# One order of all engines for a whole encoder block, in place of a framework's order and a local planner

## The chip, the cores and the metric

The kernel runs on one NeuronCore of a Trainium2 chip. Five engines work side by side, each through its own queue of instructions, in order: TensorE (PE: matmuls and transposes), VectorE (DVE), ScalarE (ACT), GpSimd (POOL) and SyncE (SP), which only issues transfers. Sixteen DMA engines move data between memory and the core. Engines wait for one another through semaphores. The metric is the device time of one execution in microseconds (us), as the median of several runs.

## The reference, cut to what matters

One block of an encoder, for 256 tokens of 2048 channels in float32, and 256 memory tokens:

```python
h = rms_norm(x, g_mix); proj = h @ w_in                      # latents (512 + 256 + 64) and dq, dk, dv (1024 each)
q = rms_norm(c_q, g_q_lat) @ w_uq; kv = rms_norm(c_kv, g_kv_lat) @ w_ukv
out_mla = mla_attention(...)                                 # 8 heads, rope on 64 channels
o_diff = diff_attention(...)                                 # 4 heads, p1 - lam * p2, then rms_norm
x = x + concat(out_mla, out_diff) @ w_out
xq = rms_norm(x, g_xattn) @ w_xq                             # cross attention, 4 heads
hm = rms_norm(mem, g_mem); xk, xv = hm @ w_xk, hm @ w_xv
x = x + softmax(xq xk^T) xv @ w_xo
hf = rms_norm(x, g_ffn)
x = x + (silu(hf @ w_gate) * (hf @ w_up)) @ w_down           # hidden width 5632
return rms_norm(x, g_final)
```

## The kernel before, in words

**Arithmetic.** Every float32 operand is split in two reduced-precision parts, high and low (`split_into`, L214): ScalarE casts the high part, VectorE subtracts it from the source to get the low part. One product is three matmuls: high by high, high by low, low by high (`mm`, L198; `mm_late`, L204, puts the products that need the low part of the weights last). A matmul has 128 by 128 weights in the array and 512 moving columns at most. Each piece of weights is loaded as float32 by SP into one of three buffers (`wraw`, 1 MB each) and split into one of four pairs of buffers (`wh`, `wl`).

**Tiling.** The 256 tokens are two row tiles (`tt`), an output column block is 512 wide (`oc`). The wide products take weights in pairs of 256 input rows by 1024 output columns. Some pairs are taken plainly ("P": 24 matmuls), some in a form with sums of blocks and seven products in place of eight ("W": 21 matmuls, more additions on VectorE). `GU_KINDS` and `DN_KINDS` say which. The sums of the weights are in `tsum`, those of the activations in `forms`; four banks q1, q5, q7, q6 gather the products, and VectorE joins them.

**Stages.** Latent projections (L546 on), attention, `w_out`, cross attention, then the FFN: a narrow chunk of 512 hidden columns (`narrow_chunk`, L1000: `ga` is the gate projection, `ua` the up projection, `sg` its SiLU, `h` the product of both, and between `ga` and `ua` `normalized_pairs` (L972) scales the transposed activations `x2T_f` by the row `rrow`, for which two transposes `rps` are made, and splits them into `x2n` and `forms`), then five wide chunks of 1024, with three down projections for them, and the final norm.

**Buffers.** Most activations live in one pool, `act`, with 24 slots of 4 KB per partition; accumulators in two pools of four banks each (`pacc`, `pps`), which change roles after each wide product (`banks.reverse()`).

**What sets the order before.** Three ways, one after the other.
- Up to and with the narrow chunk, the framework's scheduler orders the instructions from the order of the source, its own model of times, and what each reads and writes. Transfers on SP are kept in the order of the source (`tc.keep_in_program_order`).
- The wide chunks are not called directly. `flow_project`, `flow_add`, `flow_chunk` (L1083 to L1342) make a list of operations by hand (`Flow.op`, L103), each with its engine, a duration from a table (`V_COLS`, `S_COLS`, L43), what it needs, and rings of buffers that it takes and gives (`Ring`, `Hold`). `Flow.emit` (L112) keeps TensorE's matmuls in the order of the source, works back from it by when each operation is wanted, and then runs a list schedule: at each step, of the operations of an engine that could start within 0.3 us of its earliest one, the one wanted first. TensorE is taken to begin 10 us after the others. The result is issued in a block in which the framework keeps the order given.
- The rest (last part of the down projection, final norm, output) is again the framework's.

POOL makes constants at the start, the rope angles, some powers (`rstd_of`, L304) and two kinds of transfers: the memory tokens (`mn`, L921, four loads of 512 KB, for the sums of squares of `mem`, which are needed to scale `xk` and `xv`), and the final gain (`gfb`, L1385).

Of the kernel before, what the change touches and what calls it, by code (L numbers as in the profile page):

```python
# [11 lines left out]
F32 = mybir.dt.float32  # L12
# [30 lines left out]
V_COLS, S_COLS = {1024: (1.136, 1.218), 512: (0.602, 0.684), 256: (0.336, 0.416), 128: (0.202, 0.282)}, \  # L43
    {1024: (0.954, 1.053), 512: (0.523, 0.621), 256: (0.265, 0.368)}
PASS, PASS_LAG, TURN, LOADED = 0.2267, 0.2, 0.108, (4.8, 2.75)

# [22 lines left out]
class Ring:  # L69


    def __init__(self, n):
        self.n, self.holds = n, []


class Hold:


    def __init__(self, ring):
        self.gives = []  # L80
        before = ring.holds[-ring.n] if len(ring.holds) >= ring.n else None
        self.after = before.gives if before else []
        ring.holds.append(self)


class Op:


    def __init__(self, engine, busy, lag, fn, need, take, transfer):
        self.engine, self.busy, self.lag, self.fn, self.transfer = engine, busy, lag, fn, transfer  # L90
        self.need, self.take = [n for n in need if n is not None], take
        self.before, self.then, self.wanted, self.ready, self.left = [], [], 1e9, 0.0, 0


class Flow:
# [4 lines left out]
    def __init__(self):  # L100
        self.ops, self.chains = [], {}

    def op(self, engine, busy, lag, fn, need=(), take=(), give=(), chain=None, transfer=0.0):  # L103
        o = Op(engine, busy, lag, fn, need, take, transfer)
        for h in give:
            h.gives.append(o)
        if chain is not None:
            self.chains.setdefault(chain, []).append(o)
        self.ops.append(o)
        return o  # L110

    def emit(self, started):  # L112
        for o in self.ops:
            o.before = [(n, True) for n in o.need] + [(g, True) for h in o.take for g in h.after]
        for chain in self.chains.values():
            for x, y in zip(chain, chain[1:]):
                y.before.append((x, False))
        for o in self.ops:
            o.left = len(o.before)
            for b, data in o.before:  # L120
                b.then.append((o, data))
        t = 0.0
        for o in self.chains["PE"]:
            o.wanted, t = t, t + o.busy
        sorted_ops, left = [o for o in self.ops if not o.left], {o: o.left for o in self.ops}
        for o in sorted_ops:
            for n, _ in o.then:
                left[n] -= 1
                if not left[n]:
                    sorted_ops.append(n)  # L130
        assert len(sorted_ops) == len(self.ops)
        for o in reversed(sorted_ops):
            for n, data in o.then:
                o.wanted = min(o.wanted, n.wanted - (o.lag + self.HANDOVER if data else 0.0))
        place = {o: i for i, o in enumerate(self.ops)}
        open_ops, free, queue = {}, dict(started), 0.0
        for o in self.ops:
            if not o.left:
                open_ops.setdefault(o.engine, []).append(o)
        for _ in self.ops:  # L140
            picked = None
            for engine, ops in open_ops.items():
                if not ops:
                    continue
                f = free.get(engine, 0.0)
                soon = min(max(f, o.ready) for o in ops) + self.CHOICE
                o = min((o for o in ops if max(f, o.ready) <= soon), key=lambda o: (o.wanted, place[o]))
                start = max(f, o.ready)
                if picked is None or start < picked[0]:
                    picked = start, o  # L150
            start, o = picked
            open_ops[o.engine].remove(o)
            free[o.engine] = start + o.busy
# [4 lines left out]
            o.fn()  # L158
            for n, data in o.then:
                n.ready = max(n.ready, end + self.HANDOVER if data else start + o.busy)  # L160
                n.left -= 1
                if not n.left:
                    open_ops.setdefault(n.engine, []).append(n)
# [17 lines left out]
@with_exitstack  # L181
def encoder_block(ctx: ExitStack, tc: tile.TileContext, a, out):
    nc = tc.nc
    PS = bass.MemoryType.PSUM
    const = ctx.enter_context(tc.tile_pool(name="const", bufs=1))
    wp = ctx.enter_context(tc.tile_pool(name="wp", bufs=3))
    act = ctx.enter_context(tc.tile_pool(name="act", bufs=24))
    sb = ctx.enter_context(tc.tile_pool(name="sb", bufs=2))
    small = ctx.enter_context(tc.tile_pool(name="small", bufs=4))
    pacc = ctx.enter_context(tc.tile_pool(name="pacc", bufs=4, space=PS))  # L190
# [177 lines left out]
    def wide_project(pairs, src, order, kinds, leave, join, closed=(0, 1), before=None, seed=None, carried=()):  # L368
# [3 lines left out]
        if seed is not None:  # L372
            for tt in range(NT):
                for oc in range(2):
                    nc.scalar.copy(out=accs[tt][oc], in_=seed(tt, oc))
# [1141 lines left out]
```

## Time and profile before

| | |
|---|---|
| median of 3 runs | 1145.73 us (1145.5 to 1145.84) |
| the profiled execution | 1144.28 us |
| its span, first to last instruction | 1142.5 us |
| TensorE busy | 1127.7 us, 99% of the span, 5360 matmuls and transposes |
| VectorE busy | 1014.8 us, 89% |
| ScalarE busy | 694.6 us, 61% |
| moved by DMA | 222.16 MB, mean 194 GB/s |
| mean granted TensorE clock | 0.996 |

Busy time is the time in which an engine has at least one instruction in work. Matmuls follow one another before the one ahead has ended, so a busy TensorE isn't always one at its full rate. Rows of the order of time show: start, length in us, engine, line, operation, output <- inputs, shape, count, and in brackets the idle time of the engine before it and what ended that. A "PEld" is a load of weights into the array. Rows of groups show: line, engine, operation, tiles, shape, count, then busy us and mean ns of one, then the idle time before them. Rows of queues show packets, MB and the share of the time of all 16 DMA engines.

### The profile page before, as it was taken

The page shows a single profiled execution, that of the slowest core. Times are in us where ns is not written, and L with a number is a line of the kernel's source. Part 1 is how long each engine was busy: PE and PEld are TensorE (multiplying, and loading weights), DVE is VectorE, ACT ScalarE, POOL GpSimd, SP SyncE. Part 2 cuts the span into 40 slices and gives each one's busy share as a digit, 9 for nine tenths or more (in the row PEclk, how much of TensorE's full clock was granted, in tenths as well). Part 3 has the DMA queues.
Part 4 walks back from the last instruction along what each step waited for, and adds up shares of the span by engine and source line. Part 5 has one row for each costly group of instructions (what it writes and reads, how often), then busy time and mean ns, then how long its engine had stood idle before and what let it go on. Part 6 is the DMA issues. An engine that isn't in the chain of part 4 may idle for free.

```text
span 1142.5 us, 14716 instructions
## 1 busy us (share of the span) xinstructions
PE 1127.7 (99%) x5360; PEld 941.6 (82%) x5360; DVE 1014.8 (89%) x1378; ACT 694.6 (61%) x999; POOL 56.4 (5%) x75
## 2 busy tenths in 40 slices
PE   9999999999999999899999999999999999999997
PEld 7888888888888888688888888888888888888876
DVE  7788766878896776999999999999999999999995
ACT  7755455567566555656675566666665665756752
POOL 4910000000001000000000000000000000000000
PEclk9999999999999999999999999999999999999999
DMA  9655333446557445455556465456455554656453
GB/s 357 245 193 187 123 127 139 178 143 232 211 225 258 148 147 184 148 184 211 197 183 223 182 221 221 158 210 221 171 204 215 190 217 183 216 219 229 166 184 129
DMA packets 35497, 222.16 MB, mean 194 GB/s; under 512 B 4320, under 2 KB 5600, under 8 KB 11104
## 3 DMA queue, kind: packets, MB, share of 16 engines
q1 hardware_dynamic: 33696, 216.60, 52.2%
q0 software_dynamic: 864, 3.15, 0.8%
q10 hardware_dynamic: 864, 1.47, 0.4%
q8 instruction: 42, 0.69, 0.2%
q14 instruction: 31, 0.25, 0.1%
HBM read 219.11 MB, written 2.10 MB: 194 GB/s over the span
## 4 chain that ended last, share of the span: by engine, by line
PE 84%; DVE 11%; issue 3%; ACT 1%; DMA 1%; POOLq 0%; POOL 0%; SPq 0%; DVEq 0%; ACTq 0%
PE acc L1042 11%; PE acc L1041 11%; PE acc L1039 11%; PE acc L200 8%; PE acc L201 8%; PE acc L202 8%; DVE wl L1053 4%; PE q L1039 3%; PE q L1042 3%; PE q L1041 3%; PE acc L207 2%; PE acc L208 2%; PE acc L210 2%; PE pt L616 1%; DVE tsum L1136 1%
## 5 line engine op out<-in xcount | busy, mean ns | idle before, releaser
L1050 ACT CAST wh<-wraw 128x1024 fp32r<-128x1024 f32 x242 | 228.2, 957 | 95.4 <-PE acc L1042 64.5
L1053 DVE TENSOR_TENSOR wl<-wraw,wh 128x1024 fp32r<-128x1024 f32 x242 | 261.1, 1100 | 5.6 <-ACT wh L1050 3.5
L217 DVE TENSOR_TENSOR wl<-wraw,wh 128x1024 fp32r<-128x1024 f32 (+3 forms) x159 | 187.0, 1187 | 57.4 <-ACT wh L216 54.7
L216 ACT CAST wh<-wraw 128x1024 fp32r<-128x1024 f32 (+3 forms) x159 | 158.9, 1012 | 118.3 <-PE acc L202 76.0
L1050 ACT CAST wh<-tsum 128x1024 fp32r<-128x1024 f32 x108 | 113.7, 1054 | 114.1 <-DVE tsum L1131 51.4
L1053 DVE TENSOR_TENSOR wl<-tsum,wh 128x1024 fp32r<-128x1024 f32 x108 | 131.7, 1220 | 6.0 <-ACT wh L1050 5.4
L1041 PE MATMUL acc<-wh,x2n_h 128*128 128x512 f32 x320 | 125.6, 392 | 3.5 <-ACT sg L1009 2.8
L1042 PE MATMUL acc<-wh,x2n_l 128*128 128x512 f32 x320 | 124.9, 390 | 0.0
L201 PE MATMUL acc<-wl,x0T_h 128*128 128x512 f32 x224 | 88.7, 396 | 0.0
L202 PE MATMUL acc<-wh,x0T_l 128*128 128x512 f32 x224 | 88.3, 394 | 0.0
L200 PE MATMUL acc<-wh,x0T_h 128*128 128x512 f32 x224 | 86.8, 396 | 0.3 <-DVE x0T_h L220 0.3
L1039 PE MATMUL acc<-wl,x2n_h 128*128 128x512 f32 x320 | 85.8, 390 | 0.0
L1041 PE MATMUL q<-wh,forms_h 128*128 128x512 f32 x216 | 84.5, 391 | 0.3 <-ACT wh L1050 0.3
L1042 PE MATMUL q<-wh,forms_l 128*128 128x512 f32 x216 | 84.2, 390 | 0.0
L1039 PE MATMUL q<-wl,forms_h 128*128 128x512 f32 x216 | 75.9, 392 | 1.1 <-DVE wl L1053 0.9
L1136 DVE TENSOR_TENSOR tsum<-tsum,wraw 128x512 f32<-128x512 f32 x108 | 74.0, 686 | 0.5
L1041 PEld LDWEIGHTS acc<-wh,x2n_h 128*128 128x128 f32 x320 | 60.4, 189 | 16.7 <-ACT sg L1009 3.2
L1042 PE MATMUL acc<-wh,hT_l 128*128 128x512 f32 x184 | 71.7, 390 | 0.0
L1041 PE MATMUL acc<-wh,hT_h 128*128 128x512 f32 x184 | 71.7, 390 | 0.0
L1042 PEld LDWEIGHTS acc<-wh,x2n_l 128*128 128x128 f32 x320 | 60.4, 189 | 12.2
L1039 PEld LDWEIGHTS acc<-wl,x2n_h 128*128 128x128 f32 x320 | 60.0, 188 | 12.4
L1041 PE MATMUL acc<-wh,forms_h 128*128 128x512 f32 x170 | 66.2, 390 | 0.0
(431 smaller groups left out, 2348.9 us busy)
## 6 DMA issues: line engine op xcount, KB each, us to landing
wraw<-in_w_gate SPq DMA_DIRECT2D x44, 1024.0 KB, 4.8
wraw<-in_w_up SPq DMA_DIRECT2D x44, 1024.0 KB, 4.8
wraw<-in_w_dn SPq DMA_DIRECT2D x41, 1024.0 KB, 4.8
wraw<-in_w_in SPq DMA_DIRECT2D x24, 1024.0 KB, 4.8
wraw<-in_w_out SPq DMA_DIRECT2D x16, 1024.0 KB, 4.8
wraw<-in_w_in_lat SPq DMA_DIRECT2D x5, 832.0 KB, 7.4
wraw<-in_w_xk SPq DMA_DIRECT2D x4, 1024.0 KB, 4.9
wraw<-in_w_xq SPq DMA_DIRECT2D x4, 1024.0 KB, 5.1
```

The lines of the kernel that those rows point to most:

```text
L200: nc.tensor.matmul(o, l.h, r.h, start=start, stop=False, skip_group_check=seeded)
L201: nc.tensor.matmul(o, l.h, r.l, start=False, stop=False, skip_group_check=seeded)
L202: nc.tensor.matmul(o, l.l, r.h, start=False, stop=stop, skip_group_check=seeded)
L207: nc.tensor.matmul(o, l.h, r.h, start=start, stop=False, skip_group_check=seeded)
L216: last_cast[0] = nc.scalar.copy(out=dst.h, in_=src).ins
L217: last_split[0] = nc.vector.tensor_tensor(out=dst.l, in0=src, in1=dst.h.bitcast(F32), op=ALU.subtract).ins
L1039: nc.tensor.matmul(o, l.h, r.l, start=False, stop=stop, skip_group_check=seeded)
L1041: nc.tensor.matmul(o, l.h, r.h, start=start, stop=False, skip_group_check=seeded)
L1042: nc.tensor.matmul(o, l.l, r.h, start=False, stop=False, skip_group_check=seeded)
L1050: nc.scalar.copy(out=dst().h, in_=src())
L1053: last_split[0] = nc.vector.tensor_tensor(out=dst().l, in0=src(), in1=dst().h.bitcast(F32), op=ALU.subtract).ins
L1136: nc.vector.tensor_tensor(out=t[:, j, :], in0=t[:, 0 if j == 2 else 2, :], in1=got["raw"][:, j, :], op=ALU.add)
```

## The change

All three ways of ordering go. `nc` in the kernel is now a `Plan`. A call such as `nc.vector.tensor_tensor(...)` is not issued but recorded (`Plan.record`) as an operation with its engine, a duration and a lag from a formula (`Plan.cost`), and its needs: each operand is a `Ref` to a tile with the mask of the elements that it touches, and an operation comes after every earlier one that touched the same elements, where one of the two writes. A tile gets a buffer only when its first operation is placed.

`Plan.emit` then makes three runs of one list scheduler.
- The first ("asked") has no due times: on each engine, the operation that can start first, and among several the one recorded first. It hands out the slots of each pool by time: a tile whose first operation is placed takes the slot that comes free first. Within the wide stage (`plan.strict`) the matmuls keep the order of the source; transposes there are free to move.
- From its result, each tile's first operations are made to wait for all operations of the tile that had the slot before.
- Then two runs with due times: TensorE's order, but for the free transposes, is that of the first run; every other operation is due when its users need it, and a list schedule as before (0.3 us of choice, 0.06 us of handover) places it. The last run issues the calls, in a block in which the framework keeps the order.

Transfers of `sync` and of `scalar` stay in the order of the source on each queue. Those of `gpsimd` have no such rule; the load of `gfb` is put behind the split recorded last before it.

The wide stage is written as direct calls again (`wide_result`, `wide_add`, `wide_chunk` through `wide_project`, which existed). Two things differ from `flow_project`: in a W pair, the product of the third block (one column block) goes through `mm`, so its high by low matmul comes second and not third; and the accumulators of a down projection are seeded behind the issue of its first load. `mn`'s loads and everything else ahead of the wide stage are called as before.

The core of the diff:

```diff
-class Ring: ...
-class Hold: ...
-class Flow: ...
+class Plan:
+    HANDOVER, CHOICE = 0.06, 0.3
+    def record(self, engine, method, args, kw):
+        out = [x for x in (kw.get("out", args[0] if args else None), kw.get("accum_out")) if isinstance(x, Ref)]
+        ins = [x for x in list(args) + list(kw.values()) if isinstance(x, Ref) and not any(x is o for o in out)]
+        busy, lag, transfer = self.cost(engine, method, out, ins, kw, args)
...
+        op.strict = engine == "tensor" and self.strict and method == "matmul"
+        op.free = engine == "tensor" and self.strict and method == "transpose"
+        for ref, writes in [(r, True) for r in out] + [(r, False) for r in ins]:
+            t, mask = ref.tile, ref.mask()
+            for m, w, other in t.past:
+                if (w or writes) and m & mask:
+                    op.after(other, not (engine == other.engine == "tensor"))
...
+    def cost(self, engine, method, out, ins, kw, args):
+        if method == "dma_start":
+            size = max(x.cols() for x in out + ins) * 512
+            return 0.86 if engine == "gpsimd" else 0.06, 2.0 + size / 375e3, size / 381e3
+        n = max([x.cols() for x in out[:1]] + ([x.cols() for x in ins[:1]] if "reduce" in method else []))
+        if engine == "tensor":
+            if method == "transpose":
+                return 0.108, 0.33, 0.0
+            return 0.0134 + n / 2400, 0.2134 + n / 2400, 0.0
+        if engine == "gpsimd":
+            t = 0.15 + n * 0.0045
+            return t, t + 0.1, 0.0
+        if engine == "vector":
...
+                t = 0.068 + n / 960
+            return t, t + 0.082, 0.0
+        t = 0.044 + 0.855e-3 * n if ins and ins[0].tile.whole else 0.092 + 0.842e-3 * n
...
+    def run(self, chain, wanted, emit):
+        asked = wanted is None
...
+        in_turn([o for o in self.order if o.strict] if asked else chain)
+        for engine in ("sync", "scalar"):
+            in_turn([o for o in self.ops if o.engine == engine and o.transfer])
...
+                    f = free.get(engine, 0.0)
+                    at = {o: max(f, ready(o)) for o in ops}
+                    soon = min(at.values()) + (0.0 if asked else self.CHOICE)
+                    o = min((o for o in ops if at[o] <= soon), key=lambda o: (0 if asked else wanted[o], o.number))
+                    picks[engine] = at[o], o
...
+    def emit(self, rounds=2):
+        starts, ended, order = self.run(None, None, False)
...
+        for n in range(rounds):
+            chain = sorted((o for o in self.order if o.engine == "tensor" and not o.free), key=lambda o: starts[o])
+            wanted = {}
+            for o in reversed(self.order):
+                wanted[o] = starts[o] if o.engine == "tensor" and not o.free else ended
+                for x, waits in o.then:
+                    wanted[o] = min(wanted[o], wanted[x] - (o.lag + self.HANDOVER if waits else 0.0))
+            starts, ended, self.order = self.run(chain, wanted, n == rounds - 1)
...
-def encoder_block(ctx: ExitStack, tc: tile.TileContext, a, out):
-    nc = tc.nc
+def encoder_block(tc: tile.TileContext, a, out):
+    nc = plan = Plan(tc)
...
-            tc.keep_in_program_order(nc.sync.dma_start(out=raw[:, k:k + step, :], in_=src[:, k:k + step, :]))
+            nc.sync.dma_start(out=raw[:, k:k + step, :], in_=src[:, k:k + step, :])
...
+            if n == 0 and seed is not None:
+                loaded = plan.ops[-1]
+                for tt in range(NT):
+                    for oc in range(2):
+                        nc.scalar.copy(out=accs[tt][oc], in_=seed(tt, oc)).after(loaded, False)
...
+    def wide_chunk(c, kinds):
+        g = wide_result(xn, a["w_gate"][c], G_ORDER, GU_KINDS)
...
+        u = wide_result(xn, a["w_up"][c], U_ORDER, GU_KINDS)
...
+            hp, xn = narrow_chunk(0)
+            plan.strict = True
...
-            nc.gpsimd.dma_start(out=gfb[c], in_=a["g_final"][:, c * 1024:(c + 1) * 1024].partition_broadcast(P))
+            load = nc.gpsimd.dma_start(out=gfb[c], in_=a["g_final"][:, c * 1024:(c + 1) * 1024].partition_broadcast(P))
+            load.after(last_split[0], False)
...
+    with tc.manual_schedule():
+        plan.emit()
```

More of the change, by code (lines that the diff above doesn't have):

```diff
@@ L86, with __init__ @@
 class Op:
-    def __init__(self, engine, busy, lag, fn, need, take, transfer):
+    def __init__(self, engine, busy, lag, fn, transfer=0.0):
         self.engine, self.busy, self.lag, self.fn, self.transfer = engine, busy, lag, fn, transfer
-        self.need, self.take = [n for n in need if n is not None], take
-        self.before, self.then, self.wanted, self.ready, self.left = [], [], 1e9, 0.0, 0
-class Flow:
-    HANDOVER, CHOICE = 0.06, 0.3
[L100 to L137, printed above, removed]
@@ L157, in emit @@
                 queue, end = begun + o.transfer, begun + o.lag
-            o.fn()
-            for n, data in o.then:
-                n.ready = max(n.ready, end + self.HANDOVER if data else start + o.busy)
+            starts[o] = start
+            ended = max(ended, end)
+            emitted.append(o)
+            if asked:
+                for h in o.tiles:
+                    if h not in placed:
+                        placed.add(h)
+                        h.old = h.slots.pop(0)[1]
+                        picks.clear()
+                    h.end = max(h.end, end + self.HANDOVER)
+                    to_go[h] -= 1
+                    if not to_go[h]:
+                        h.slots.append((h.end, h))
+                        h.slots.sort(key=lambda x: x[0])
+                        picks.clear()
@@ L161, in emit @@
+            if emit and o.fn is not None:
+                o.fn()
+            for n, waits in o.then:
+                if waits:
+                    t = end if n.engine == o.engine or n.engine == "none" else end + self.HANDOVER
+                else:
+                    t = start + o.busy
+                n.ready = max(n.ready, t)
                 n.left -= 1
                 if not n.left:
-                    open_ops.setdefault(n.engine, []).append(n)
+                    opened(n)
+            for n in queued.get(o, ()):
+                n.ready = max(n.ready, start + o.busy)
+                n.left -= 1
+                if not n.left:
+                    opened(n)
@@ L538, in encoder_block @@
     x0T = Transposed(a["xT"], g_mix, "x0T",
[L539 removed]
+                     lambda: nc.sync.dma_start(out=gains, in_=a["gains"]))
     w_in = a["w_in"]
```

625 lines of the change are left out of this document (272 added, 353 removed).

## The prediction, made before the changed kernel was run

> **What bounds the kernel now.** I read the page first (busy times, then the chain of waits), then the table of stretches, then the order of time where a stretch falls short. The profiled execution took 1144.28 us, its span 1142.5, so 1.8 lie around the span. It is 1.45 under the median of the runs (1145.73); I work out a change against the profile and add it to the median.
>
> ```profile
> span 1142.5 us, 14716 instructions
> PE 1127.7 (99%) x5360; PEld 941.6 (82%) x5360; DVE 1014.8 (89%) x1378; ACT 694.6 (61%) x999; POOL 56.4 (5%) x75
> PE 84%; DVE 11%; issue 3%; ACT 1%; DMA 1%; POOLq 0%; POOL 0%; SPq 0%; DVEq 0%; ACTq 0%
> ```
>
> TensorE sets the end. All that an order can win is its idle time, 14.8 us by this row, plus what it loses while counted as busy. Where that lies (columns: stretch, length, then busy us and records of PE, PEld, DVE, ACT, POOL, granted clock, DMA share, GB/s):
>
> ```profile
> 0.00:50.00 50.00, 48.45 (x239) 40.34 (x240) 35.99 (x51) 36.81 (x66) 34.06 (x45) 1.00 0.85 320
> 50.00:100.00 50.00, 50.00 (x313) 44.99 (x312) 42.98 (x76) 29.28 (x47) 12.49 (x16) 1.00 0.52 184
> 450.00:487.00 37.00, 32.48 (x140) 25.72 (x139) 32.98 (x54) 22.09 (x35) 0.00 (x0) 0.95 0.39 142
> 600.00:700.00 100.00, 100.00 (x442) 82.86 (x442) 95.90 (x106) 57.15 (x63) 0.00 (x0) 1.00 0.56 204
> 700.00:800.00 100.00, 100.00 (x451) 83.11 (x450) 99.46 (x116) 64.35 (x78) 0.00 (x0) 1.00 0.57 206
> 1050.00:1100.00 50.00, 49.65 (x223) 39.90 (x221) 49.86 (x72) 34.32 (x52) 0.00 (x0) 1.00 0.47 168
> 1135.40:1142.50 7.10, 0.02 (x1) 0.00 (x0) 2.19 (x6) 1.34 (x2) 0.55 (x1) 0.65 0.60 223
> ```
>
> Only one stretch inside the kernel falls short: 450 to 487, the passage from the narrow FFN chunk to the wide ones. The start and the 7.1 us of epilogue are the rest. In the wide stage VectorE is as full as TensorE (99.46 of 100). The passage in order of time:
>
> ```profile
> 454.28 0.38 PE L978 MATMUL rps<-ident,rb 128*128 128x128 f32 x2
> 454.41 0.48 PE L200 MATMUL acc<-wh,x2T_h 128*128 128x512 f32 x1
> ...
> 456.70 4.62 DVE L982 TENSOR_TENSOR x2T_f<-x2T_f,rrow 128x1024 f32<-128x1024 f32 x4
> ...
> 477.50 0.39 PE L202 MATMUL acc<-wh,x2T_l 128*128 128x512 f32 x1
> ...
> 479.97 0.69 ACT L1009 ACTIVATE sg<-acc,x2Tr 128x512 f32<-128x512 f32 x1 [0.96 <-DVE forms_l L217]
> ...
> 480.71 0.50 PE L1041 MATMUL acc<-wh,x2n_h 128*128 128x512 f32 x1 [2.82 <-ACT sg L1009]
> ...
> 482.46 1.11 PE L616 MATMUL pt<-ident,h 128*128 128x128 f32 x4 [1.02 <-DVE h L1011]
> ...
> 484.25 1.11 PE L616 MATMUL pt<-ident,h 128*128 128x128 f32 x4
> ```
>
> The second SiLU (sg) reads an accumulator that has been complete since ga ended, yet it stands behind the forms_h splits in ScalarE's queue; the bank that it frees is what the first gate matmul waits for. From 456.70 on VectorE has x2T_f, all pairs and the weights at once.
>
> **The change part by part.** No engine call is added or dropped: the split by transfer that goes had no caller, and recording is host work. What changes is order alone, so each part is a stall that goes or comes.
>
> *The passage (450 to 487).* Its 140 records at the undisturbed rate: 130 matmuls at 0.226 (100.00 us over x442) and 10 transposes at 0.109 (row below, 1.75 over 16) make 30.5; 6.5 of 37.0 are lost. With one due time for everything, sg goes as soon as ScalarE is free, the banks come free one by one, and forms that the gate's order uses late are split late. The limit is VectorE from 457 to the next stall at 593.6:
>
> ```profile
> 717.18 1.75 PE pt L1260 x16
> 457.00:593.60 136.60, 131.49 (x583) 107.60 (x581) 131.80 (x174) 88.33 (x114) 0.00 (x0) 0.99 0.50 180
> ```
>
> It worked 131.80 of 136.60, so without moving work ahead of 457 at most 4.8 can be won by 593.6. Work can hardly move ahead: everything waits on rrow, its transposes (rps) stand on TensorE after ga's matmuls at 454.28, and TensorE's order in the new plan is that of its first run, where the lowest recorded number goes first; ga is recorded ahead of rps. Bounds: 0 (VectorE merely stalls later) to 4.8. I take -4.3: 0.5 of idle time will remain.
>
> *The start, POOL's queue.* Now the four loads of mem (tile mn, L921) stand late in the kernel, at 344.69:
>
> ```profile
> 344.69 2.40 POOL L921 DMA_DIRECT2D mn<-in_mem  x4
> ...
> 1.04 0.29 POOL masks.py:199 TENSOR_SCALAR_AFFINE_SELECT ident<-ident 128x128 f32<-128x128 f32 x1
> 13.85 0.19 POOL L568 CAST posf<-posi 128x2 f32<-128x2 int32 x1 [12.52 <-DMA posi<-in_pos]
> ...
> q1 hardware_dynamic: 553, 4.01, 51.3%
> q0 software_dynamic: 576, 2.10, 31.4%
> ```
>
> In the plan they need nothing but a free act slot: the source isn't a recorded tile, only sync and scalar transfers are kept in turn, and no `after` holds them as one now holds gfb. A list schedule never lets an engine stand while something is ready, and POOL is free from 1.33 to 13.85. At the start about nine of 24 act slots are taken. So I expect mn's loads at about 2 us, moved past all of POOL's later work. The last two rows are the queues from 340 to 360, where mn ran: 2.10 MB took 31.4% of 20 us on all 16 engines, 6.3 us of the whole DMA. At the start there is no room for it:
>
> ```profile
> 5.00:10.00 5.00, 4.70 (x23) 3.85 (x24) 3.85 (x9) 3.40 (x7) 0.00 (x0) 1.00 1.01 362
> 30.00:35.00 5.00, 5.00 (x28) 4.41 (x27) 3.67 (x7) 4.91 (x13) 4.53 (x6) 1.00 0.99 391
> 35.00:40.00 5.00, 5.00 (x29) 4.46 (x28) 4.60 (x4) 2.58 (x4) 4.75 (x4) 1.00 0.59 202
> 17.07 1.68 ACT L216 CAST wh<-wraw 128x832 fp32r<-128x832 f32 x2 [2.31 <-DMA wraw<-in_w_in_lat]
> 18.65 0.91 ACT L222 ACTIVATE x0T_h<-xraw,gains 128x256 fp32r<-128x256 f32 x2
> 19.34 0.39 PE L200 MATMUL acc<-wh,x0T_h 128*128 128x512 f32 x1
> ```
>
> The DMA is full from 5 to 35. ScalarE waits 2.31 us for the weights of the seventh k-tile, casts from 17.07, and TensorE uses them at 19.34. The least from landing to use is one cast and one activation, half of 1.68 and half of 0.91, 1.3; so the slack there is 2.27 - 1.3, 1.0. Weights that land 6.3 late stall TensorE 5.3; if the queues share evenly and the earlier k-tiles take part of it, a little less. Bounds: 0 (not moved) to 6.3. I take +5.0. Nothing downstream gives it back, because TensorE is full to 450. ScalarE's eight squares of mn come early too, in its idle time (36.81 of 50).
>
> [...]
>
> *Durations that the plan has too low.* Its formula gives a POOL pow 0.16 us; the trace has
>
> ```profile
> L309 POOL TENSOR_TENSOR rd<-rd,mhalf 128x2 f32<-128x2 f32 x4 | 2.8, 700 | 170.2 <-DVE rd L308 170.2
> ```
>
> 0.70, so transposes that follow rq, rkv, rd and the others may stand 0.5 too early in TensorE's fixed order. Some ten such places: 0 to 5. I take +0.5: in the front part matmuls of the projections lie ready around them (50.00 of 50.00 busy from 50 to 100), and ScalarE and VectorE have 20 to 40% idle.
>
> *The wide stage after 593.6.* Same calls, the same method, the same handover of 0.06 and choice of 0.3; formulas in place of a table (512 columns on VectorE 0.601 for 0.602). Where TensorE stalls (49.65 of 50), VectorE is full (49.86), so order wins little: 0, from -1 to +2. Here lie the small edits: in a summed piece's single product the low weights are wanted one matmul (0.226) earlier, covered while VectorE leads; transposes go one by one, at no cost (454.28 to the matmul's 454.41 and on); gfb's loads start behind a split. The epilogue is one chain of one tile: 0.
>
> Sum: -4.3 + 5.0 + 0.5 + 0 = **+1.2 us**; the profile would take 1145.5, the median **1146.9**. Its own range: the passage 0 to -4.8, the start 3.8 to 6.3, the rest as bounded, rarely all on one side: 1143.5 to 1150. What this kernel's measurement can tell from no change is 0.2%, 2.3 us: 1143.4 to 1148.0.
>
> **Rivals.**
> *The loads of mem do no harm*: they are issued elsewhere, or the weights in flight keep ahead of them. Then -4.3 + 0.5 = -3.8, **1141.9**. For it: they go through another queue than the weights, and how the two share the engines at the start no row shows. Against it: the DMA share of 1.0 to 35 us, where whatever is added must push something, and the slack of 1.0.
> *VectorE takes the gain back* (slower): the forms that are put off past 487 meet a VectorE that is full, and the stall of 593.6 grows by what the passage lost. Then +5.0 + 0.5, **1151.2**. It decides if VectorE's 4.8 us of idle time from 457 to 593.6 stays, for instance because the weight buffers are full at the wrong time. For it: 99% busy from 700 on. Against it: the order of the passage itself, where an engine with finished input (sg) waits in a queue.
> *The clock drops in the starved start.* After the gap before 480.71 four transposes took 1.11 where sixteen take 1.75, and the granted clock of 450 to 487 is 0.95. If short waits behind each k-tile do the same, about 2 us of matmuls at half rate come on top: +3.2, **1148.9**. Against it: the waits would be near 1 us each, not 2.82 in one. [...]
> *The order is not followed* (the framework reorders): **1145.7**.
>
> **How the numbers follow.** Chances: forecast 0.39, harmless loads 0.33, VectorE takes it back 0.15, clock 0.08, order not followed 0.05. Range 1140.5 to 1151.5: from 1.4 under the harmless case (half the small stalls of the wide stage gained as well) to just past the VectorE case. Faster: 0.32 of the harmless case and 0.01 of the forecast, 0.33. Slower: 0.12 of the forecast (the start at 6.3, or ten late pows), 0.14 of VectorE's, 0.06 of the clock's, 0.32. Same: the rest, 0.35.
>
> **What would show it.** Right: mn's loads on POOL before 5 us, DMA full beyond 40, ScalarE's waits on w_in_lat several us longer in sum, TensorE about 5 short in the first 50; then sg well ahead of ua's last matmul, no wait over 1 us before the first gate matmul, its clock at 1.00, and VectorE over 99% busy from there to the first down projection. Wrong: mn's loads past 300 us, or TensorE full in the first 50 although they are early; a stall near the end of the first down projection of 3 us and more; new waits of TensorE between 50 and 450 that sum to over 2 us.

## The result and the profile after

The changed kernel takes 1153.01 us (median of 4 executions, 1152.72 to 1153.24) against 1145.72 for the kernel before in the same comparison: **ratio 1.0064, 95% interval 1.0046 to 1.0081**, 7.3 us slower. The prediction was 1146.9 with a range of 1140.5 to 1151.5, so the time lies outside it, on the slow side. The profiled execution took 1153.09 us, its span 1151.2; the span of before was 1142.5. The 8.7 us between the spans are what has to be explained; they are more than the 7.3 between the medians because the profiled execution of before was 1.45 under its median.

The page of the changed kernel, busy times and then the shares of the chain of waits:

```profile
span 1151.2 us, 14663 instructions
PE 1132.5 (98%) x5360; PEld 941.0 (82%) x5360; DVE 1017.4 (88%) x1378; ACT 695.4 (60%) x999; POOL 54.8 (5%) x75
PE 81%; DVE 10%; POOL 4%; ACT 2%; issue 2%; DMA 1%; SPq 0%; POOLq 0%; DVEq 0%; ACTq 0%
```

The 5360 TensorE instructions are the same. TensorE stood idle for 18.7 us (14.8 before) and was counted busy for 4.8 us more with the same work, so some of it took longer. POOL, which hardly showed on the chain of before (0%), now has 4% of it. In stretches (stretch, length, busy us and records of PE, PEld, DVE, ACT, POOL, granted clock, DMA share, GB/s):

```profile
0.00:50.00 50.00, 45.94 (x210) 36.52 (x211) 30.93 (x44) 36.30 (x71) 31.64 (x44) 1.00 0.92 343
50.00:100.00 50.00, 49.10 (x297) 43.65 (x297) 40.42 (x72) 31.10 (x53) 16.68 (x22) 1.00 0.50 183
100.00:150.00 50.00, 49.35 (x306) 43.47 (x305) 40.72 (x86) 27.10 (x59) 0.00 (x0) 1.00 0.31 106
150.00:200.00 50.00, 49.47 (x250) 41.25 (x249) 36.90 (x67) 27.09 (x53) 1.42 (x2) 1.00 0.45 156
...
350.00:400.00 50.00, 48.79 (x254) 40.88 (x253) 38.44 (x62) 26.66 (x44) 0.69 (x1) 1.00 0.45 164
450.00:495.00 45.00, 44.52 (x202) 36.61 (x201) 34.76 (x50) 27.46 (x39) 0.69 (x1) 1.00 0.48 169
```

The passage (last row) is nearly full now, where before it was 32.48 of 37. The start has 29 instructions fewer in its first 50 us, and the front part, full to 400 us before, falls short in all four of its rows here.

To have one measure for waits and for slow steps, I add up by how much the distance between the starts of two neighbouring TensorE instructions exceeds the usual distance for that shape in the traces (0.227 us for 512 columns, 0.147 for 320, 0.120 for 256, 0.109 for a transpose; a shorter distance counts as negative, and the first column begins with the first product). The sums in us, per section of the kernel, for every kernel of this study:

| kernel | 0 to 50 | 50 to 450 | 450 to 605 | after 605 | sum | first product starts | last starts before the end |
|---|---|---|---|---|---|---|---|
| before | 0.9 | 2.5 | 7.6 | 2.5 | 13.5 | 5.25 | 7.33 |
| changed | 6.6 | 8.3 | 3.3 | 2.8 | 20.9 | 5.99 | 7.86 |
| e1 loads held | 0.7 | 11.1 | 3.5 | 2.8 | 18.1 | 5.87 | 7.86 |
| e2 three durations | 6.4 | 4.4 | 3.3 | 2.8 | 16.9 | 5.99 | 7.86 |
| e3 both | 1.0 | 6.2 | 3.3 | 2.9 | 13.4 | 6.32 | 7.86 |
| e4 before, loads early | 5.2 | 2.5 | 8.4 | 2.4 | 18.5 | 6.16 | 7.33 |
| e5 power alone | 6.4 | 6.8 | 3.3 | 2.7 | 19.2 | 5.86 | 7.86 |
| e6 Exp alone | 5.9 | 7.3 | 3.3 | 3.1 | 19.6 | 6.24 | 7.87 |
| e7 both, order free | 0.9 | 4.5 | 3.3 | 2.8 | 11.5 | 5.92 | 7.87 |
| e8 before, Silu early | 1.4 | 2.5 | 10.2 | 2.4 | 16.6 | 5.06 | 7.33 |
| e9 changed again | 6.3 | 8.2 | 3.3 | 2.7 | 20.6 | 5.90 | 7.85 |
| e10 before, h ahead of 4 pairs | 0.8 | 2.5 | 5.2 | 3.1 | 11.6 | 5.13 | 7.34 |
| e11 before, h ahead of 2 pairs | 0.7 | 2.5 | 5.2 | 3.0 | 11.4 | 5.02 | 7.34 |
| e12 power at 1.6 | 0.6 | 2.9 | 3.5 | 2.8 | 9.8 | 5.80 | 7.86 |

Changed against before: start +5.7, front +5.8, passage -4.3, rest +0.3, the first product 0.7 later, the tail 0.5 longer: 8.7, the difference of the spans. So two losses of the same size stand against one gain, and only one of the two was in the prediction at anything like its size.

**The start.** In the changed kernel every instruction is issued from one line, L224, so its rows are told apart by their tiles. In order of time, POOL first:

```profile
1.23 2.29 POOL L224 DMA_DIRECT2D mn<-in_mem  x4 [0.80 <-POOLq L1446]
```

and TensorE:

```profile
6.56 0.63 PE L224 MATMUL acc<-wl,x0T_h 128*128 128x512 f32 x1
8.81 0.63 PE L224 MATMUL acckv<-wh,x0T_h 128*128 128x320 f32 x1 [1.63 <-ACT wh L224]
9.34 0.63 PE L224 MATMUL acckv<-wl,x0T_h 128*128 128x320 f32 x1
9.77 0.63 PE L224 MATMUL acc<-wh,x0T_h 128*128 128x512 f32 x1
10.20 0.63 PE L224 MATMUL acc<-wh,x0T_l 128*128 128x512 f32 x1
...
13.40 0.41 PE L224 MATMUL acc<-wh,x0T_l 128*128 128x512 f32 x1
...
16.36 0.50 PE L224 MATMUL acc<-wl,x0T_h 128*128 128x512 f32 x1 [0.57 <-DVE wl L224]
```

and ScalarE:

```profile
7.69 0.63 ACT L224 ACTIVATE junk<-mn 128x512 bf16<-128x512 f32 x1 [2.83 <-DMA mn<-in_mem]
...
8.32 0.44 ACT L224 CAST wh<-wraw 128x320 fp32r<-128x320 f32 x1
...
10.81 0.98 ACT L224 CAST wh<-wraw 128x512 fp32r<-128x512 f32 x2 [1.03 <-DMA wraw<-in_w_in_lat]
```

The four loads of mem go out from 1.23 us on. One wait of 1.63 us for the cast of weights at 8.32 follows. That cast is late because ScalarE's order is kept too: a square of mn stands ahead of it and waited 2.83 us for mn to land. The next cast, at 10.81, waits for the weights themselves. Matmuls of 512 columns start 0.43 us apart (9.77, 10.20) in place of 0.227, until 13.40. They were no faster before the wait: the one at 6.56 is 0.63 long as well, where the same shape takes 0.39 later. From 9.34 to 13.40 these half-rate steps alone cost 2.0 us; with the step after 8.81 and the waits they make most of the 5.7.

**The front.** Of the waits of TensorE that the kernel before didn't have, these are shown, in order of time (all of the changed kernel):

```profile
67.39 0.44 PE L224 MATMUL pt<-ident,ckv 128*128 128x128 f32 x2 [0.90 <-DVE gT L224]
...
179.45 0.39 PE L224 MATMUL pod<-val_h,pT_h 128*128 128x256 f32 x1 [0.53 <-ACT pT_h L224]
...
255.41 0.30 PE L224 MATMUL pdt<-ident,on 128*128 128x128 f32 x1 [0.28 <-DVE on L224]
...
396.92 0.30 PE L224 MATMUL ppt<-ident,e 128*128 128x128 f32 x1 [1.21 <-DVE e L224]
```

Each is a transpose (pt, pdt, ppt) or a short product (pod) of the attention whose input or bank is late, and behind it in TensorE's queue stand matmuls of a projection that could have run: the one behind pod started at 179.79, and the last cast of weights that ended ahead of it was done at 178.90 (177.85 + 1.05; the next began at 179.26 and took 1.08).

**The passage.** In order of time, ScalarE's two SiLU, and then TensorE from the last product of ua on:

```profile
467.33 0.69 ACT L224 ACTIVATE sg<-acc,x2Tr 128x512 f32<-128x512 f32 x1
...
469.12 0.70 ACT L224 ACTIVATE sg<-acc,x2Tr 128x512 f32<-128x512 f32 x1
```

```profile
488.27 0.39 PE L224 MATMUL acc<-wh,x2T_l 128*128 128x512 f32 x1
488.49 0.39 PE L224 MATMUL acc<-wh,x2n_h 128*128 128x512 f32 x1
...
490.04 0.66 PE L224 MATMUL pt<-ident,h 128*128 128x128 f32 x4 [0.47 <-DVE h L224]
...
601.42 0.50 PE L224 MATMUL q<-wl,forms_h 128*128 128x512 f32 x1 [0.93 <-DVE wl L224]
```

Both SiLU are done 18 us ahead of the last product of ua, the first gate matmul follows it without a wait, and the wait near the end of the first down projection grew only from 0.59 to 0.93.

### The profile page after: what moved, and what is told of

Its sections match the earlier page's. It is cut to its first block, busy times and chain, and to the rows that moved or that the text cites. A ratio compares the mean times of both kernels' runs of the same rounds, so it can differ in the third digit from the quotient of the medians.

```text
span 1151.2 us, 14663 instructions
## 1 busy us (share of the span) xinstructions
PE 1132.5 (98%) x5360; PEld 941.0 (82%) x5360; DVE 1017.4 (88%) x1378; ACT 695.4 (60%) x999; POOL 54.8 (5%) x75
## 4 chain that ended last, share of the span: by engine, by line
PE 81%; DVE 10%; POOL 4%; ACT 2%; issue 2%; DMA 1%; SPq 0%; POOLq 0%; DVEq 0%; ACTq 0%
PE acc L224 63%; PE q L224 13%; DVE wl L224 3%; PE pt L224 2%; POOL prod L224 1%; DVE res L224 1%; PE qT L224 1%; DMA wraw<-in_w_in_lat 1%; POOL ang L224 1%; DVE tsum L224 1%; POOL turns L224 1%; DVE nm L224 1%; PE psc L224 1%; DVE sums L224 1%; DVE forms_l L224 1%
## 5 line engine op out<-in xcount | busy, mean ns | idle before, releaser
L224 DVE TENSOR_TENSOR wl<-wraw,wh 128x1024 fp32r<-128x1024 f32 (+2 forms) x401 | 449.2, 1133 | 92.2 <-ACT wh L224 90.7
L224 ACT CAST wh<-wraw 128x1024 fp32r<-128x1024 f32 (+2 forms) x401 | 388.0, 978 | 234.7 <-PE acc L224 192.3
L224 ACT CAST wh<-tsum 128x1024 fp32r<-128x1024 f32 (+1 forms) x118 | 119.5, 1017 | 127.4 <-DVE tsum L224 73.7
L224 DVE TENSOR_TENSOR wl<-tsum,wh 128x1024 fp32r<-128x1024 f32 (+1 forms) x118 | 137.9, 1174 | 5.8 <-PE acc L224 4.0
L224 PE MATMUL acc<-wh,x2n_h 128*128 128x512 f32 x320 | 124.7, 390 | 0.0
L224 PE MATMUL acc<-wh,x2n_l 128*128 128x512 f32 x320 | 124.6, 389 | 0.0
L224 PE MATMUL q<-wh,forms_h 128*128 128x512 f32 x231 | 91.4, 396 | 1.4 <-ACT res L224 1.4
L224 PE MATMUL q<-wh,forms_l 128*128 128x512 f32 x231 | 90.0, 390 | 0.0
L224 PE MATMUL acc<-wl,x0T_h 128*128 128x512 f32 x224 | 89.2, 398 | 0.6 <-DVE wl L224 0.6
L224 PE MATMUL acc<-wh,x0T_h 128*128 128x512 f32 x224 | 89.0, 397 | 0.6 <-DVE x0T_h L224 0.6
L224 PE MATMUL acc<-wh,x0T_l 128*128 128x512 f32 x224 | 88.6, 395 | 0.0
L224 PE MATMUL acc<-wl,x2n_h 128*128 128x512 f32 x320 | 86.1, 390 | 0.0
L224 PE MATMUL q<-wl,forms_h 128*128 128x512 f32 x231 | 81.0, 392 | 1.1 <-DVE wl L224 1.1
L224 DVE TENSOR_TENSOR tsum<-tsum,wraw 128x512 f32<-128x512 f32 x118 | 80.7, 684 | 0.8
L224 PE MATMUL acc<-wh,forms_l 128*128 128x512 f32 x192 | 74.9, 390 | 0.0
L224 PE MATMUL acc<-wh,forms_h 128*128 128x512 f32 x192 | 74.9, 390 | 0.0
L224 DVE TENSOR_TENSOR tsum<-wraw 128x1024 f32<-128x1024 f32 (+1 forms) x64 | 72.2, 1134 | 1.5 <-DMA wraw<-in_w_out 1.5
L224 PE MATMUL acc<-wh,hT_h 128*128 128x512 f32 x188 | 73.4, 390 | 0.0
L224 PE MATMUL acc<-wh,hT_l 128*128 128x512 f32 x188 | 73.2, 389 | 0.0
L224 PE MATMUL acc<-wl,forms_h 128*128 128x512 f32 x192 | 72.9, 390 | 0.0
L224 PEld LDWEIGHTS acc<-wh,x2n_l 128*128 128x128 f32 x320 | 60.1, 188 | 12.5
L224 PEld LDWEIGHTS acc<-wh,x2n_h 128*128 128x128 f32 x320 | 60.1, 188 | 12.5
```

The source lines that it names most:

```text
L224: getattr(getattr(self.tc.nc, engine), method)(*[made(x) for x in args], **{k: made(x) for k, x in kw.items()})
```

## The experiments

Three questions: is the start's loss the loads of mem or the order that the plan gives the start; does the front's loss come from durations that the plan has too low, or from TensorE's order, which is kept from the first pass; and what made the passage faster. Times are medians, ratios are to the kernel before on the same chips.

**Loads held (e1).** The loads wait for a late POOL instruction, the power of rstdx:

```
...
-            nc.gpsimd.dma_start(out=mn, in_=a["mem"][tt * P:(tt + 1) * P, c * 1024:(c + 1) * 1024])
+            load = nc.gpsimd.dma_start(out=mn, in_=a["mem"][tt * P:(tt + 1) * P, c * 1024:(c + 1) * 1024])
+            load.after(last_pow[0], False)
```

> The changed kernel with one difference: the four loads of mn are issued only after the last POOL power that precedes them in the source (rstdx), as g_final's loads already wait for a DVE instruction. Theory 1 (the start pays for 2.10 MB that travel among the first weights): the whole 5.0 to 6.5 us of the first 50 us come back, 1146.5 to 1148.0 us. Rival (the start lost its time to the order the plan gives the first splits and matmuls, the loads are harmless): 1152.0 to 1153.5 us. Between the two if half of the loss is the clock that fell in the starved start and falls without the loads too: about 1150 us.

Measured: 1148.68 us, ratio 1.0037 (1.0024 to 1.0050). That is 0.7 above what was expected if the loads were all of it. The start is clean (0.7 lost for 6.6), so the loads are its whole loss of 0 to 50 us, by their traffic and by the squares of mn that move with them. But less came back than was lost, since the front now loses 11.1 for 8.3. The traced execution took 1150.19, 1.5 over the median, so the median one loses less there than these rows show:

```profile
62.61 0.44 PE L224 MATMUL pt<-ident,ckv 128*128 128x128 f32 x2 [2.06 <-DVE gT L224]
...
64.11 0.63 PE L224 MATMUL acc<-wl,x0T_h 128*128 128x512 f32 x1
```

and the stretch after that wait:

```profile
62.60:67.00 4.40, 4.39 (x14) 3.54 (x15) 3.98 (x7) 1.75 (x4) 0.00 (x0) 0.61 0.06 15
```

TensorE is free for the transposes of ckv 5.9 us earlier (60.55 for 66.49), but what they wait for (DVE's gT, behind POOL's power of rkv) is done only 4.8 us earlier (62.61 for 67.39). So the wait grows from 0.90 to 2.06, and matmuls at half rate follow, here with a granted clock of 0.61 in the stretch.

**Three durations corrected (e2), and both (e3).** In the plan's formula of costs:

```
-            t = 0.15 + n * 0.0045
+            t = 0.6 if kw.get("op") == ALU.pow else 0.15 + n * 0.0045
...
-                t = 0.07
+                t = 0.1
...
-            t += 0.093
+            t += 0.093 if n > 256 else 0.19
```

> The changed kernel with three durations of the plan set to what its own trace shows: a POOL power 0.60 us (was 0.15), an Exp with its accumulator read 0.45 us (was 0.356), a DVE instruction of two columns 0.10 us (was 0.07). The loads of mn stay at the start. Theory 2 (new waits of TensorE between 50 and 450 us, 5.7 us in sum, come from durations that the plan has too low): 4 to 6 us come back, 1147.0 to 1149.0 us; the power alone would be worth about 2.7, the Exp about 2.2 of it. Rival (TensorE's order is fixed by the first pass, which ranks by the source, and the durations only shift idle time): 1152.0 to 1153.5 us.

> Both differences at once. If start and front are separate places on the path, the gains add: 1141.0 to 1143.0 us, which is the time before less the 4.4 us that the passage after the gate projections gained. If one hides the other (the front only has slack because the start was late), the better of the two alone: 1147 us. If neither theory holds: 1152 to 1153.5 us.

Measured: e2 1148.94 us, ratio 1.0034 (1.0021 to 1.0046); e3 1144.33 us, ratio 0.9999 (0.9990 to 1.0008). The three numbers take 3.9 of the front's 5.8 us away (8.3 to 4.4) and nothing elsewhere. With the held loads as well the changed kernel is level with the kernel before. The changed kernel itself stands at 1152.3 on this comparison (1144.90 by the ratio 1.0065 of its second measurement below), so e1 gave 3.7, e2 3.4 and both 8.0: the gains add. The expectation, the time before less the passage's 4.4, was missed because in e3 the front still loses 3.7 us more than before and the first product starts 1.1 later. Both are of the traced execution, which took 1145.76, 1.4 over e3's median.

**The loads alone, in the kernel before (e4).** The order of before, and four loads as POOL's first instructions, into buffers nothing reads:

```
+    for tt in range(NT):
+        for c in range(2):
+            idle = act.tile([P, 1024], F32, name="idle", tag="act")
+            tc.keep_in_program_order(nc.gpsimd.dma_start(
+                out=idle, in_=a["mem"][tt * P:(tt + 1) * P, c * 1024:(c + 1) * 1024]))
```

> The kernel before, its order untouched, with four more loads of the rows of mem issued by POOL as its first instructions, into buffers that nothing reads (this adds 2.10 MB; the output is the reference's). Theory 1: the first weights land later by what 2.10 MB take, 1150.5 to 1152.0 us against 1145.7. Rival (only the plan's order of the start is late, loads harmless): 1145.5 to 1146.5 us.

Measured: 1150.42 us against 1144.90, ratio 1.0049 (1.0035 to 1.0063): +5.5 us. With no plan involved the loads cost what the changed kernel loses at its start. In the traced execution the start has 4.3 us of it, the first product starts 0.9 later and the passage loses 0.8 more. The wait falls elsewhere: the rows loaded here are not squared, so ScalarE's cast waits 2.12 us for the weights alone. Since it starts at 10.43, and the same cast in the changed kernel at 10.81, the late landing of the weights is what both kernels pay for. TensorE's wait of 2.45 us and matmuls of 512 columns 0.43 us apart (12.65, 13.08) in place of 0.227 follow:

```profile
10.43 0.98 ACT L216 CAST wh<-wraw 128x512 fp32r<-128x512 f32 x2 [2.12 <-DMA wraw<-in_w_in_lat]
```

```profile
11.10 1.22 PE L200 MATMUL acc<-wh,x0T_h 128*128 128x512 f32 x2 [2.45 <-ACT wh L216]
...
12.65 0.63 PE L201 MATMUL acc<-wl,x0T_h 128*128 128x512 f32 x1
13.08 0.63 PE L202 MATMUL acc<-wh,x0T_l 128*128 128x512 f32 x1
```

**One duration at a time (e5, e6).** Only the line of the power, or only that of the Exp, of e2's edit.

> The changed kernel with one duration of the plan corrected, POOL's power (0.60 us, was 0.15). All three corrected durations together gave 3.3 us. If the power is most of it, as the step on durations of the prediction had it: 2.0 to 3.3 us below the changed kernel, 4.0 to 5.3 us above the kernel before of the same chip, and the waits of the transposes pdt on DVE's on near 255 us are gone. If the Exp carries it: under 1 us below the changed kernel.

> The changed kernel with one duration of the plan corrected, the Exp with its accumulator read (0.45 us, was 0.356). If the Exp carries the new waits of the attention: 2.0 to 3.0 us below the changed kernel, and the waits of po, ppt and pod near 114, 128 and 179 us are gone. If the power is most of it: under 1 us below the changed kernel, those waits stay.

Measured: e5 1151.24 us, ratio 1.0057 (1.0044 to 1.0069); e6 1152.15 us, ratio 1.0064 (1.0051 to 1.0077), where the changed kernel has 1.0065. Both expectations failed: the power gives about 1 us, the Exp nothing that can be told, and together (with the two-column instructions) they gave 3.4. Where they fell short can be seen: e5 loses the wait at 67 us and keeps those of po, ppt and pod; e6 keeps the one at 67 and trades those of 114 and 128 for new ones, and the transposes of pdt wait longer than in the changed kernel:

```profile
126.28 0.41 PE L224 MATMUL pt<-ident,dn 128*128 128x128 f32 x2 [0.46 <-DVE dn L224]
...
184.09 0.30 PE L224 MATMUL pdt<-ident,on 128*128 128x128 f32 x1 [0.93 <-DVE on L224]
```

As I read it (no run shows it by itself), a plan that still has one duration wrong moves work into the room that this duration pretends to have. The two-column instructions of VectorE have no run of their own, so part of the 3.4 may be theirs.

**TensorE's order set free (e7).** On top of e3, outside the wide stage:

```
-            chain = sorted((o for o in self.order if o.engine == "tensor" and not o.free), key=lambda o: starts[o])
+            chain = sorted((o for o in self.order if o.strict), key=lambda o: starts[o])
```

> Held loads and corrected durations, and TensorE's order outside the wide stage is chosen anew in each round by slack instead of being kept from the first pass (only the matmuls of the wide stage stay in that order). If the kept order is what still stalls TensorE between 50 and 450 us (5.9 us lost there with held loads and corrected durations, against 2.4 in the kernel before): 2 to 3 us below that kernel, 1141.5 to 1142.5 us for a kernel before of 1144.9. If those waits are chains that no order of TensorE avoids: within 0.8 us of it.

Measured: 1143.20 us, ratio 0.9988 (0.9979 to 0.9997). The gain over e3 is 1.1 us, between the two expectations; the intervals of the two ratios overlap, so its size is uncertain. The transposes of ppt near 390 us waited in e3 (first row) and don't in e7 (second), so that wait came from the kept order; those of ckv and pdt still wait.

```profile
390.05 0.30 PE L224 MATMUL ppt<-ident,e 128*128 128x128 f32 x1 [0.97 <-ACT pxT_h L224]
```

```profile
389.78 0.30 PE L224 MATMUL ppt<-ident,e 128*128 128x128 f32 x1
```

**The passage, one part alone (e8).** In the kernel before, the SiLU ahead of the pairs:

```
         ga = project(x2T, [a["w_gate0"][0, i] for i in range(4)])
+        sg = act.tile([P, NT, 512], F32, name="sg", tag="act")
+        for tt in range(NT):
+            nc.scalar.activation(sg[:, tt, :], ga[tt], AF.Silu, scale=rstdf[:, tt:tt + 1])
         xn = normalized_pairs()
...
-            sg = nat("sg")
-            nc.scalar.activation(sg, ga[tt], AF.Silu, scale=r)
```

> The kernel before with one part of the change alone: the two Silu of the narrow gate are issued right behind the gate projection, ahead of the normalized pairs, into one buffer of the act ring. If the Silu's place in ACT's order is the passage's loss: 4.0 to 4.8 us below the kernel before (1140.1 to 1140.9 for 1144.9). If VectorE, busy for 131.80 of 136.6 us there, takes it back: 0 to 1 us below, with DVE the releaser of new TensorE waits before the first down projection ends.

Measured: 1147.19 us, ratio 1.0019 (1.0010 to 1.0027): slower, by about 2 us. Neither expectation holds; the passage loses 10.2 for 7.6:

```profile
482.17 0.66 PE L616 MATMUL pt<-ident,h 128*128 128x128 f32 x4 [2.87 <-DVE h L1012]
...
485.76 0.69 PE L616 MATMUL pt<-ident,h 128*128 128x128 f32 x2 [2.48 <-DVE h L1012]
```

The wait for sg is gone, and both waits for VectorE's h have grown, from 1.02 and none. A wait of 1.33 us for VectorE's wl at 474 is new as well. VectorE has the sums of all the pairs and most of their low halves ahead of h in its queue.

**The changed kernel again (e9)**, as the comparison for what ran beside it:

> The changed kernel itself, on the chip of this call, so that the others can be set against it: 7 to 8 us above the kernel before. If the chips differ in what they make of it, the earlier comparisons with 1153.0 have to be read again by ratios to the kernel before.

Measured: 1152.81 us against 1145.17, ratio 1.0065 (1.0052 to 1.0078): as before.

**VectorE's order too (e10, e11).** On top of e8 the pairs are recorded in the order in which the first gate product uses them, and the last ones of it behind h (e10 four of eight, e11 two):

```
...
         xn = normalized_pairs()
+        add_pairs(xn, (0, 2, 1, 4))
...
             transposed(t, h, tt, 4)
+        add_pairs(xn, (3, 6, 7, 5))
```

> The kernel before with the Silu early and, in addition, the pairs that the first gate product uses last (3, 6, 7, 5 of its order) recorded behind the two products h, so that VectorE reaches h ahead of their splits. With the Silu early alone TensorE waited 2.87 and 2.48 us for DVE's h. If VectorE's order is the other half of the passage's gain: 3.5 to 5.0 us below the kernel before. If the passage is bound by VectorE's total work: within 1 us of it or slower, with the waits moved to a later wl.

> As the kernel before with early Silu and reordered pairs, but only the last two pairs (7 and 5) stand behind h. If h's place in VectorE's queue sets the wait, this lies between: h comes later by two pairs' work (about 2.5 us of VectorE by its instructions of 0.6 and 0.34 us), 1 to 3.5 us below the kernel before. If the total work bounds it: the same as with four pairs behind h.

Measured: e10 1142.44 us, ratio 0.9976 (0.9966 to 0.9986); e11 1142.08 us, ratio 0.9974 (0.9963 to 0.9984). They are three us below the kernel before, and five below e8. The gain of e10, 2.7, is less than the 3.5 to 5.0 expected. So VectorE's order around h is the second part of the passage; whether it is h's place or the order of the pairs, which changed with it, these runs do not separate. That e11 isn't slower than e10 speaks for the second reading of e11's expectation and against h's place alone: TensorE waits longer for h (2.67 us, the row stands in the last section, for 1.55), but waits that follow in e10 are gone (0.73 us at 492 and 0.30 at 515), and both lose 5.2.

```profile
478.77 0.66 PE L616 MATMUL pt<-ident,h 128*128 128x128 f32 x4 [1.55 <-DVE h L1017]
```

**The power as it is beside VectorE (e12).** On top of e7, 1.6 in place of 0.6 for the power.

> Held loads, corrected durations, TensorE's order free, and POOL's power set to 1.6 us in the plan, which is what it takes beside a VectorE split of 1024 columns (1.63 and 1.70 us in the kernel with 0.6 in the plan, 0.55 to 0.73 without such a split). If those long powers are behind the waits of pt on ckv (62 us) and pdt on on (177 us): both waits gone, 0.8 to 1.7 us below the kernel with 0.6. If not: within 0.4 us of it.

Measured: 1141.86 us, ratio 0.9973 (0.9963 to 0.9984), 1.7 us below e7 by the ratios. Both waits are gone, the front loses 2.9 (before 2.5):

```profile
50.00:100.00 50.00, 50.00 (x321) 45.40 (x321) 42.80 (x78) 31.84 (x54) 12.54 (x15) 1.00 0.49 176
150.00:200.00 50.00, 50.00 (x257) 42.23 (x256) 39.10 (x74) 27.34 (x53) 2.32 (x2) 1.00 0.46 163
```

The change with held loads, three right durations and a free order outside the wide stage is thus faster than both kernels, by 0.27% than the one before.

## Why the prediction was wrong

**Durations that the plan has too low: +0.5 taken, +5.8 measured in the front where they act. This is the step that failed.** The bounds were 0 to 5, and the choice near 0 rested on two reasons: that matmuls of the projections lie ready around the places, and that ScalarE and VectorE have idle time. The first is no help in an order that is fixed: the transposes of ckv, 0.90 us late at 67.39, and pod, 0.53 late at 179.45, held what stood behind them in TensorE's queue, ready or not. I had argued just so for sg on ScalarE. The prediction's own sign of this, new waits of TensorE between 50 and 450 us, came out at 3.97 us of idle time for 0.20 before. And the list of durations was too short. I looked at the power only; rows of ScalarE in the changed kernel show another one, though correcting it alone gave nothing that can be told (e6):

```profile
172.89 0.47 ACT L224 ACTIVATE e<-psc,nm 128x256 f32<-128x256 f32 x1
173.25 0.20 ACT L224 ACTIVATION_READ_ACCUMULATOR e<-psc,nm 128x1 f32 x1
173.34 0.47 ACT L224 ACTIVATE e<-psc,nm 128x256 f32<-128x256 f32 x1
```

An Exp with the read of its sum starts every 0.45 us (172.89, 173.34); the plan has 0.356, four of them in a row. What the runs give for the 5.8: 3.9 go with the three durations (e2). With the loads held as well the front stands at 6.2 (e3), because the early loads had covered part of the wait at ckv; the free order takes 1.7 of that (e7), the power at 1.6 us another 1.6 (e12), which leaves 0.4 over before. These are sums of traced executions; by the medians the free order gives 1.1. So not all of the 5.8 is durations: the wait of ppt (1.21 us at 396.92) stays with the three corrected (0.96 in e2) and goes with the free order, and that order, kept from the first pass, had no term in the sum.

**The start: +5.0 taken, +5.7 measured (e1 and e4 show that it is the loads); right in mechanism.** Its make-up was different. I had 5.3 us of weights that land late; the waits are 1.63 and 0.57, and half-rate steps are at least 2.0. I also put the squares of mn into ScalarE's idle time, at no cost; in the fixed order one of them held the first of these waits, though e4 shows that the late weights cost as much without it. The rival "the clock drops" had that mechanism as an addition of 2 us with a chance of 0.08. It isn't an addition: it is part of the price. In the profiled execution the matmul ahead of the wait (6.56, 0.63 long) was as slow as those behind it. In e2, whose loads go out as early, the granted clock over the first 25 us reads 0.93 for 1.00 here, and the start loses 6.4 for 6.6; in the second measurement (e9) it loses 6.3. POOL's queue moved 29.6% of the DMA time of the first 20 us (5.9 us for the 2.10 MB, the row of before gave 6.3). The lower end of 3.8 us that the range gave this term no run shows: the start lost 5.7 us more than before in the changed kernel and 4.3 in e4.

**The passage: -4.3 taken, -4.3 measured; right in size, half right in cause.** The prediction named the place of sg in ScalarE's queue. e8 shows that this alone loses 2 us, and e10 and e11 that a change of VectorE's order is needed too. They bring the passage's loss from 7.6 to 5.2, and the changed kernel brings it to 3.3; the rest of its gain no run separates, so the agreement in size is partly luck. Of the 7.6 before, about 1.6 are matmuls at half rate behind the wait of 2.82 us (granted clock 0.50 from 482.16 to 485.57). In the changed kernel and e10 the clock reads 1.00 from 450 to 495, in e11 from 470 to 485. In the changed kernel the last splits of x2n and forms come at 496 us, behind both h; the prediction said "forms that the gate's order uses late are split late", but priced only sg. The rival in which VectorE takes the gain back fell: the wait near the end of the first down projection is 0.93.

**What was set to 0.** The wide stage +0.3, within its -1 to +2. The epilogue +0.5 and the first product +0.7 were not in the sum. The latter stays in every kernel of the plan with the loads held (5.80 to 6.32), so it is not theirs; which of the plan's choices makes it, or makes the epilogue longer, no run here separates.

**The rivals.** Harmless loads: refuted by e4 (+5.5 us). Order not followed: refuted by the row of mn at 1.23 us. With the measured 5.8 in place of 0.5 the sum would have been -4.3 + 5.0 + 5.8 = +6.5, 1152.2 on the median, against 1153.0.

## What to carry to other kernels

When one fixed order of all engines replaces the orders of a framework and a local planner, a duration that the order's model has too low can become a wait on the engine that sets the end (here three of them made 3.9 of the front's 5.8 us), so compare each formula with the trace's groups (the pairs of instructions that belong together too) before trusting the order. A transfer that no due time holds goes to the front (here from 344.69 us to 1.23; the same loads cost the kernel before 5.5 us); hold it. And a stall that goes with one queue's order may only move to the next engine's (in e8 from ScalarE's sg to VectorE's h, 2.87 and 2.48 us): look at which engine holds the same step second.

## What the runs showed of the hardware

**The half rate after a wait.** The length of the wait alone does not decide here. After waits of 2.06 us (e1) and 2.45 (e4) matmuls ran at half rate for about 3.4 us, 0.43 us apart in place of 0.227: the granted clock is 0.50 from 63.46 to 66.88 in e1 (0.61 over 62.60 to 67.00) and from 11.04 to 14.45 in e4 (0.93 over the first 25 us). After 2.67 us in e11 the next ones of 512 columns came at the full rate, 0.23 apart (0.32 beside a transpose):

```profile
480.02 0.66 PE L616 MATMUL pt<-ident,h 128*128 128x128 f32 x4 [2.67 <-DVE h L1017]
...
482.81 0.39 PE L1048 MATMUL acc<-wh,x2n_h 128*128 128x512 f32 x1
483.05 0.39 PE L1049 MATMUL acc<-wh,x2n_l 128*128 128x512 f32 x1
```

In e11 the granted clock reads 1.00 from 470 to 485. What decides between the two cases no run here shows.

**Half rate without a drop.** In the starts of the changed kernel and of e6 the half rate was there before the wait. In e6 the wait is 0.90 us, and the matmul at 6.81 is as long as those after it:

```profile
6.81 0.63 PE L224 MATMUL acc<-wl,x0T_h 128*128 128x512 f32 x1
8.34 0.64 PE L224 MATMUL acckv<-wh,x0T_h 128*128 128x320 f32 x1 [0.90 <-ACT wh L224]
...
9.30 0.63 PE L224 MATMUL acc<-wh,x0T_h 128*128 128x512 f32 x1
```

In the changed kernel matmuls of 512 columns come 0.43 us apart up to 13.40 and 0.23 apart from 14.09 on, in e6 0.43 apart still at 12.50 and 12.93; in the kernel before they come 0.23 apart from 6.62 on. So in these two starts the full rate came late, and they say nothing of the wait after which the rate falls. In the changed kernel's start the granted clock reads 1.00 all the same; the first clock that its trace records begins at 13.42 us, and the column counts as full what lies before. There the distances of the starts have to be read, not that column:

```profile
10.00:15.00 5.00, 5.00 (x19) 4.23 (x19) 1.65 (x4) 2.12 (x4) 0.00 (x0) 1.00 1.04 400
```

**POOL's power beside a VectorE subtraction.** The same instruction on two columns took 0.70 us or 1.63. In e7, POOL and then VectorE in order of time:

```profile
175.22 1.63 POOL L224 TENSOR_TENSOR rd<-rd,mhalf 128x2 f32<-128x2 f32 x1 [91.14 <-DVE rd L224]
177.91 0.70 POOL L224 TENSOR_TENSOR rd<-rd,mhalf 128x2 f32<-128x2 f32 x1 [1.06 <-DVE rd L224]
```

```profile
175.04 1.22 DVE L224 TENSOR_TENSOR wl<-wraw,wh 128x1024 fp32r<-128x1024 f32 x1
176.88 0.88 DVE L224 SCALAR_TENSOR_TENSOR on<-pod,rd,gdb 128x256 f32<-128x256 f32 x2 [0.62 <-POOL rd L224]
```

The long one began 0.18 us after a VectorE subtraction of 1024 columns and ended 0.59 after that one's end (175.04 + 1.22 = 176.26, 175.22 + 1.63 = 176.85), as if it had started only then. Why, no run shows. In e12 the first power of rd took 1.63 again (174.05) and the second 0.70 (176.75). The plan of e7 has 0.6 for each, and e12, whose plan allows 1.6 for every power, is 1.7 us faster than e7.
